# One layer of a state-space and pooling mixer on one core: the zero fill of the Toeplitz scratch placed behind the x loads, the pool groups from window 16 to window 2, and new places of issue

## The chip, the cores and the metric

The kernel runs on one core of a Trainium2 chip. Four engines compute: TensorE (PE, matmuls and transposes), VectorE (DVE), ScalarE (ACT) and GpSimd (POOL). SyncE (SP) issues every DMA of this kernel, in one queue. The metric is the device time of one execution in microseconds (us); less is better.

## What is computed

The reference is one layer with two mixers that read the same input. In short (2048 prompt rows and 8 sample rows of 1024 values, 512 columns to each mixer, 32 ssm groups of 16 channels with 64 complex states each):

```
proj = h @ w_in                                   # 1024 -> 2048
s_in, s_gate, p_in, p_gate = split(proj)          # 512 columns each
sy, hr, hi = s5_mixer(s_in, h0, ...)              # h_t = a*h_(t-1) + bbar*u_t ; y = Re(c*h) + d*u
sy = gelu(sy)
sy = sy * sigmoid(sy @ glu_w + glu_b)
py = pool_mixer(p_in, prefix)                     # per window w in (2, 4, 8, 16): mean of the last w rows
                                                  # minus the row; @ pool_w[group] ; * pool_scale
mixed = concat([sy * silu(s_gate), py * silu(p_gate)])
y = layer_norm(alpha * h + mixed @ w_out)
```

The outputs are y for the prompt and the sample rows, the new ssm states, and the last 15 rows of p_in.

## The kernel before

**Stages.** All large products are float32 products made of three passes of a high and a low part (hi by hi, hi by lo, lo by hi). x is loaded in 17 row tiles (`load_x`), transposed on PE and split into a high part `xh` (cast on ACT) and a low part `xl` (subtraction on DVE) by `put_x`. The in-projection `proj` (L200) makes 16 column tiles of 128: 0 to 3 are the ssm input (`u_tile`, L541), 4 to 7 its gates (`gate`), 8 to 11 the pool inputs (`pool_in`, L822) and 12 to 15 the pool gates (`pool_gate`). Each runs over chunks of 512 or 256 rows. `u_tile` copies its product on ACT to a tile `ue` and stores that to DRAM (`u_d`), from which the ssm stage reads it again by groups. There are two `ue` buffers, so the ACT copy waits until an earlier store has landed.

**The tables.** The state-space recurrence is done as block-Toeplitz products. The task `params` (L226) works the parameters up on DVE: exponentials, sines and cosines (tiles `tr`, `zs`), then powers (`prv`), and then eight blocks of two group pairs each (loop at L409). Each block has four products `sp` and two sums on DVE (L419 to L425), a PE part into `ps_ks` (L429 to L440, two small products and four transposes of `sp`), a split `sv` stored to `sw_d`, a sum `kf` split into `kv`, and a split `qh` stored to `qw_d`. After every second block eight DMAs write `kv` into `wt_d`, the Toeplitz scratch (L457 to L461). `wt_d` has to hold zeros in its other half, so `params` fills it before the blocks: a memset of the tile `wzero` on POOL and four DMAs of 1 MB (L375 to L380). The task `tables` (L464) makes the tables `tb` and `tx` for the ssm stage beside it. `ssm_task` (L678) waits until `params` and `tables` have ended, and then does 16 group pairs: it loads their tables and inputs, makes `uh`, and issues the products `s` and `y` on PE, with a scan on DVE (`B`, `hf`) and a copy on POOL (`bus`).

**The pooling.** For each of the four groups (tile numbers gi 0 to 3 have windows 2, 4, 8, 16) and each of five row chunks, `pool_in` puts the product into a tile `pc`, and the task `pool_diff` (L839) builds the sum over the window by doubling: log2(window) additions on POOL (tiles `ws`), then a difference `df` on DVE, and a split `dh` (cast on ACT, subtraction on DVE). `pool_gate` multiplies it on PE with the group's pool weights (`pm`) and stores the result to `mp_d`. The first three groups run beside the end of the ssm stage (loop at L925), the last one beside the GLU product `z` and the preparation of the output weights `wo` and of `mix`, the input of the output product `o`.

**What sets the order.** A hand-written order: each compute engine executes its instructions in the order in which the program records them. A class `Line` keeps a virtual clock; `proj` advances it after every three matmuls by the time they should take, and then lets every task run that is due. Tasks are generators, and `yield 3.0` says that the next piece is due 3.0 virtual us later. So the many numbers behind `yield`, and the start delays in `line.add`, decide only between which matmuls the next piece of work is recorded. The order of SP's DMAs is set by a scheduler from that program.

Of the kernel before, what the change touches and what calls it, by code (L numbers as in the profile page):

```python
# [17 lines left out]
P = 128  # L18
# [22 lines left out]
HT = HC // 2  # L41
CHUNKS_U = ((0, 256, 0), (256, 256, 0), (512, 512, 0), (1024, 512, 0), (1536, 256, 0), (1792, 256, NB))
# [60 lines left out]
def hybrid_step(  # L103
# [122 lines left out]
    def params(tmp, prod):  # L226
# [10 lines left out]
        yield 4.80  # L237
# [16 lines left out]
        yield 0.80  # L254
# [6 lines left out]
        def expo(out, z, shape, nm):  # L261
# [6 lines left out]
            yield 0.69  # L268
# [3 lines left out]
            yield 0.96  # L272
# [43 lines left out]
        yield 2.50  # L316
        V.tensor_scalar(out=acc, in0=r2, scalar1=-1.0 / math.factorial(14), scalar2=None, op0=ALU.mult)
        for i in (12, 10, 8, 6, 4, 2):
            if i == 6:
                yield 1.30  # L320
            V.scalar_tensor_tensor(out=acc, in0=acc, scalar=(-1.0) ** (i // 2) / math.factorial(i), in1=r2, op0=ALU.add, op1=ALU.mult)
        V.scalar_tensor_tensor(out=zs[:, 0], in0=acc, scalar=1.0, in1=sgn, op0=ALU.add, op1=ALU.mult)
        yield 2.50
# [23 lines left out]
        yield 0.84  # L347
# [19 lines left out]
        yield 1.00  # L367
# [7 lines left out]
        z = prod.tile([P, 512], F32R, tag="hl", name="wzero")  # L375
        G.memset(z.bitcast(F32), 0.0)
        for j in range(0, 8, 2):
            dma(out=wt_d[j:j + 2].rearrange("j a c g h o -> (j a c g h o)").rearrange("(p x o) -> p x o", x=4, o=512),
                in_=z.bitcast(F32).unsqueeze(1).to_broadcast([P, 4, 512]))
        yield 0.60  # L380
# [28 lines left out]
        for g0 in range(0, GP, N2):  # L409
# [17 lines left out]
            while not tabs:  # L427
                yield 0.50
# [28 lines left out]
            if (g0 + N2) % NG == 0:  # L457
                gs = slice(g0 + N2 - NG, g0 + N2)
# [4 lines left out]

    def tables():  # L464
        while "table" not in ready or "x" not in ready:
            yield 0.58
        zs = shared["zs"]
        for q in range(4):
# [3 lines left out]
            for lv in range(6):  # L472
# [6 lines left out]
                yield (1.20, 0.71, 0.79, 1.00, 0.74, 2.20)[lv]  # L479
            tx = tabs[0].tile([P, 2, 4, HT], F32, tag="tx", name=f"tx{q}")  # L480
            ms = tabs[0].tile([P, 2, 4, HT], F32, tag="mt", name="ms")
            for g in range(4):
# [4 lines left out]
                yield 0.60  # L487
# [87 lines left out]
    tab = line.add(tables(), 10.00)  # L575

    def x_task():
        for i in range(2, 17):
# [4 lines left out]
            yield 2.88 if i > 2 else 1.10  # L583
# [6 lines left out]
    xg = line.add(x_task(), 0.80)  # L590
# [18 lines left out]
    w3 = line.add(w_in_task(3, 2.48))  # L609
# [4 lines left out]
    line.add(w_in_task(4, 1.12))  # L614
# [63 lines left out]
    def ssm_task():  # L678
        while any(x[1] in (par, tab) for x in line.tasks):
            yield 0.09  # L680
# [13 lines left out]
        yield 0.51  # L694
# [4 lines left out]
        yield 2.40  # L699
# [69 lines left out]
        yield 5.86  # L769
# [52 lines left out]
    def pool_in(gi, c):  # L822
# [10 lines left out]
        ptasks.append(line.add(pool_diff(gi, c, pc), 0.14))  # L833
# [3 lines left out]
    def pool_diff(gi, c, pc):  # L837
# [9 lines left out]
        yield 0.98 + 1.22 * (len(bin(w)) - 3) * n / 512  # L847
# [24 lines left out]
    def pool_gate(gi, c):  # L872
        t0, n, s = c
        g = silu2(proj(12 + gi, c), n, s, f"p{gi}_{t0}")
        while (gi, t0) not in dfs:
            yield 0.24
# [6 lines left out]
        yield 1.00  # L883
# [15 lines left out]
    sg = line.add(ssm_task(), 0.50)  # L899
    gt = pw_sb = rcnt = sps = None  # L900
    for m in range(4):
# [6 lines left out]
        nxt = (6, 7, 8, 12)[m]  # L908
# [338 lines left out]
```

## Time and profile before

| | us |
|---|---|
| time, median of 3 runs | 711.62 (709.89 to 712.07) |
| the profiled execution's own time | 713.83 |
| its span in the trace | 711.9 |
| PE busy | 684.9 |
| DVE busy | 490.4 |
| ACT busy | 237.3 |
| POOL busy | 194.3 |
| mean granted clock of PE | 0.987 |

The busy time of an engine counts its instructions and not its waits, and it is a mean over stages with different limits. A table by stretches shows busy time, granted clock and DMA share for each stage; the waits of an engine say which instruction ended its idle time; a timeline shows single instructions, and in brackets how long the engine had stood idle before one and what released it.

### The profile page before, as it was taken

The numbers are of one execution on the slowest core, as the hardware profiler recorded it, in microseconds if no ns is written. First come the engines' busy times: TensorE is split into PE (matmuls) and PEld (weight loads), VectorE is DVE, ScalarE is ACT, GpSimd is POOL, SyncE is SP. The second block draws the span as 40 slices with busy tenths as digits, with TensorE's granted clock in tenths as the row PEclk, the third lists the DMA queues.
The fourth block names the chain that finished last, engine by engine and source line by source line (L and its number), as shares of the span: only waits on it lengthen the run. The fifth ranks groups of instructions, "written<-read, shape, count | busy, mean of one in ns | idle before, by whom it ended". The sixth has DMA issues, their size and how long they took to land.

```text
span 711.9 us, 10836 instructions
## 1 busy us (share of the span) xinstructions
PE 684.9 (96%) x3763; PEld 580.3 (82%) x3763; DVE 490.4 (69%) x1002; ACT 237.3 (33%) x490; POOL 194.3 (27%) x251
## 2 busy tenths in 40 slices
PE   7989889999999999999999999989999999999995
PEld 6978778878888888988987887776888868888884
DVE  3589989862665787687888973686655577666444
ACT  4244333331343343344334332363221323232100
POOL 0104554410000021022224213763314234153222
PEclk9999999999999999999999999999999999999998
DMA  8994477777654544344444325945354552752432
GB/s 252 289 333 111 112 190 206 170 211 216 189 159 137 162 132 125 111 146 142 127 145 129 107 90 133 358 138 106 103 120 121 112 143 74 177 160 72 111 88 59
DMA packets 138069, 107.95 MB, mean 152 GB/s; under 512 B 74467, under 2 KB 115591, under 8 KB 138007
## 3 DMA queue, kind: packets, MB, share of 16 engines
q1 hardware_dynamic: 137855, 107.01, 53.5%
q8 instruction: 29, 0.48, 0.3%
q10 hardware_dynamic: 160, 0.26, 0.1%
q14 instruction: 25, 0.20, 0.1%
HBM read 64.74 MB, written 42.73 MB: 151 GB/s over the span
## 4 chain that ended last, share of the span: by engine, by line
PE 71%; DVE 7%; ACT 3%; DMA 2%; SPq 2%; issue 1%; DVEq 0%; POOL 0%; ACTq 0%; POOLq 0%
PE pj L212 34%; PE o L1116 24%; PE z L1076 5%; PE y L669 2%; PE y L739 2%; PE s L654 2%; PE pm L880 1%; SPq L460 1%; PE os L1116 1%; DVE tx L486 1%; DMA wst<-in_w_in_dram 1%; DVE mix L150 1%; DVE wo L150 1%; DMA u_d<-ue 1%; DVE sp L150 1%
## 5 line engine op out<-in xcount | busy, mean ns | idle before, releaser
L212 PE MATMUL pj<-xh,w 128*128 128x512 f32 (+2 forms) x1312 | 335.4, 349 | 2.6 <-ACT w L156 2.6
L212 PEld LDWEIGHTS pj<-xh,w 128*128 128x128 f32 x1312 | 226.2, 191 | 32.6 <-ACT w L156 3.1
L212 PE MATMUL pj<-xl,w 128*128 128x512 f32 (+2 forms) x656 | 209.0, 350 | 0.0
L1116 PE MATMUL o<-wo,mix 128*128 128x512 f32 (+1 forms) x792 | 178.2, 386 | 1.5 <-ACT mix L156 1.5
L1116 PEld LDWEIGHTS o<-wo,mix 128*128 128x128 f32 x792 | 146.1, 189 | 32.7 <-ACT mix L156 2.5
L212 PEld LDWEIGHTS pj<-xl,w 128*128 128x128 f32 x656 | 121.7, 192 | 15.3
L150 POOL TENSOR_TENSOR xr<-xr,gb 128x1024 f32<-128x1024 f32 x15 | 37.0, 2470 | 48.5 <-DVE xr L150 35.5
L150 POOL TENSOR_TENSOR ws<-pc 128x527 f32<-128x527 f32 (+1 forms) x20 | 19.5, 977 | 106.5 <-ACT pc L831 57.9
L1076 PE MATMUL z<-yh,w_g 128*128 128x512 f32 (+2 forms) x240 | 45.1, 347 | 0.0
L1076 PEld LDWEIGHTS z<-yh,w_g 128*128 128x128 f32 x240 | 38.7, 189 | 5.9
L1105 ACT ACTIVATE xr<-xr,mv 128x1024 f32<-128x1024 f32 x15 | 18.7, 1244 | 74.2 <-DVE mv L1095 72.8
L713 POOL COPY bus<-SP 128x16 f32<-128x16 f32 x16 | 8.6, 535 | 119.9 <-ACT SP L707 119.8
L1084 DVE SCALAR_TENSOR_TENSOR xr<-xr,o 128x512 f32<-128x512 f32 (+1 forms) x33 | 22.0, 667 | 27.0 <-PE o L1116 27.0
L150 POOL TENSOR_TENSOR ws<-ws 128x525 f32<-128x525 f32 (+5 forms) x30 | 34.0, 1133 | 3.3 <-DVE dh L150 1.1
L150 DVE TENSOR_TENSOR xl<-pt,xh 128x1024 fp32r<-128x1024 f32 (+2 forms) x19 | 20.0, 1057 | 20.7 <-ACT xh L156 20.6
L150 DVE TENSOR_TENSOR yh<-y,yh 128x512 fp32r<-128x512 f32 (+2 forms) x20 | 13.9, 693 | 23.5 <-ACT yh L156 23.5
L150 POOL TENSOR_TENSOR mv<-mv,mhalf 128x1 f32<-128x1 f32 x16 | 9.9, 619 | 72.8 <-DVE mv L1090 69.5
L707 ACT COPY SP<-s 64x264 f32<-64x264 f32 x64 | 23.9, 373 | 17.3 <-PE s L654 16.8
L791 DVE SCALAR_TENSOR_TENSOR g<-g,pj 128x512 f32<-128x512 f32 (+1 forms) x20 | 11.6, 578 | 23.5 <-ACT g L790 23.5
L150 DVE TENSOR_TENSOR xr<-xr,gb 128x1024 f32<-128x1024 f32 x15 | 19.7, 1314 | 10.5 <-ACT xr L1105 10.5
L150 DVE TENSOR_TENSOR mix<-y,mix 128x512 fp32r<-128x512 f32 (+2 forms) x20 | 18.0, 901 | 12.7 <-ACT mix L156 12.7
L156 ACT CAST xh<-pt 128x1024 fp32r<-128x1024 f32 (+2 forms) x19 | 16.7, 884 | 26.4 <-PE pt L147 24.9
(222 smaller groups left out, 891.2 us busy)
## 6 DMA issues: line engine op xcount, KB each, us to landing
wst<-in_w_in_dram SPq DMA_DIRECT2D x15, 512.0 KB
xr<-in_x_prompt_dram SPq DMA_DIRECT2D x24, 256.0 KB
out_dram<-xr SPq DMA_DIRECT2D x22, 256.0 KB
xw<-in_x_prompt_dram SPq DMA_DIRECT2D x8, 512.0 KB
wt_d<-wzero SPq DMA_DIRECT2D x4, 1024.0 KB
sw_d<-sv SPq DMA_DIRECT2D x8, 512.0 KB
qw_d<-qh SPq DMA_DIRECT2D x16, 256.0 KB
ws<-sw_d SPq DMA_DIRECT2D x16, 256.0 KB
```

The lines of the kernel that those rows point to most:

```text
L150: (eng or V).tensor_tensor(out=out, in0=a, in1=b, op=op)
L156: S.copy(out=hi, in_=src)
L212: nc.tensor.matmul(out=ps[:, :n], lhsT=w[:, a, k], rhs=xcols(b, k, t0, n), start=(i == 0), stop=(i == 23))
L654: nc.tensor.matmul(out=ps[:, c, 0:264], lhsT=ws[:, c, a], rhs=uh[:, b, c, 8:272], start=(i == 0), stop=(i == 2))
L669: nc.tensor.matmul(out=py[:, c, 0:264], lhsT=wq[cs, r, a], rhs=hh[cs, b, r], start=False, stop=(i == 5))
L707: S.copy(out=SP[64 * c:64 * c + 64, a], in_=ps[64 * a:64 * a + 64, c, 0:264])
L739: nc.tensor.matmul(out=py[:, c, 0:264], lhsT=wt[:, c, a], rhs=uh[:, b, c, 0:264], start=(i == 0), stop=False)
L791: V.scalar_tensor_tensor(out=g[:, :n], in0=g[:, :n], scalar=1.0, in1=jm(ps[:, :n]), op0=ALU.add, op1=ALU.mult)
L1076: nc.tensor.matmul(out=ps[:, :n], lhsT=w[:, a, k, P * (m % 2):P * (m % 2) + P], rhs=yh[:, b, k, :n], start=(i == 0), stop=(i == 11))
L1084: V.scalar_tensor_tensor(out=xt[:n, c], in0=xt[:n, c], scalar=ALPHA, in1=ps, op0=ALU.mult, op1=ALU.add)
L1105: S.activation(out=xt[:n], in_=xt[:n], func=AF.Identity, scale=mv[:n, 2:3], bias=mv[:n, 0:1])
L1116: nc.tensor.matmul(out=ps, lhsT=lhs(a, k), rhs=wo_view(k)[:, b, 512 * h + c.start:512 * h + c.stop], start=(i == 0), stop=(i == len(hl) * ...
```

## The change

The change has three parts.

1. The zero fill is taken out of `params` and becomes a task of its own, `zeros`. It starts when all x tiles are put, takes its zero tile from a pool that is opened then, and issues the four fills 3.93 virtual us apart. The first `wt_d` write from `kv` waits (in the virtual order) for it, and `ssm_task` waits for its end.
2. The pool groups come in the order of `PG`: window 16, 8, 4, 2. The weights' loads follow that order, and the group beside the GLU product is now the one of window 2.
3. Some 45 numbers behind `yield` and of start delays are new.

```diff
+PG = (3, 2, 1, 0)
@@ params
-        z = prod.tile([P, 512], F32R, tag="hl", name="wzero")
-        G.memset(z.bitcast(F32), 0.0)
-        for j in range(0, 8, 2):
-            dma(out=wt_d[j:j + 2]..., in_=z...)
-        yield 0.60
+        yield 0.66
...
             while not tabs:
-                yield 0.50
+                yield 0.35
...
             if (g0 + N2) % NG == 0:
+                while "zeros" not in ready:
+                    yield 0.03
                 gs = slice(g0 + N2 - NG, g0 + N2)
...
+    def zeros():
+        while "x" not in ready:
+            yield 0.76
+        z = tabs[0].tile([P, 512], F32, name="wzero")
+        G.memset(z, 0.0)
+        for j in range(0, 8, 2):
+            dma(out=wt_d[j:j + 2]..., in_=z...)
+            yield 3.93
+        ready["zeros"] = True
...
-                yield (1.20, 0.71, 0.79, 1.00, 0.74, 2.20)[lv]
+                yield (1.11, 0.65, 0.70, 1.31, 0.74, 2.27)[lv]
...
-    PY = (5.08, 3.00, 2.20)
+    PY = (5.04, 3.00, 2.20)
...
+    zer = line.add(zeros(), 6.26)
-    tab = line.add(tables(), 10.00)
+    tab = line.add(tables(), 10.66)
...
-    w3 = line.add(w_in_task(3, 2.48))
+    w3 = line.add(w_in_task(3, 0.98))
...
-        while any(x[1] in (par, tab) for x in line.tasks):
+        while any(x[1] in (par, tab, zer) for x in line.tasks):
@@ pools
-        yield 0.98 + 1.22 * (len(bin(w)) - 3) * n / 512
+        yield 0.73 + 1.27 * (len(bin(w)) - 3) * n / 512
...
-        nxt = (6, 7, 8, 12)[m]
+        nxt = (6, 7, 8 + PG[0], 12 + PG[0])[m]
...
-    for gi in range(3):
+    for gi, ng in zip(PG, PG[1:]):
...
-    pool_seq(3, ((1, 0), (0, 0), (1, 1), ...), hook)
+    pool_seq(PG[3], ((1, 0), (0, 0), (1, 1), ...), hook)
@@ output stage
-        yield 5.43 if ck else 13.90
+        yield 13.07 if ck else 14.63
...
-            yield 2.70 if ck else 6.72
+            yield 0.14 if ck else 6.72
...
-        yield 7.00
+        yield 4.13
         yield from wo_split(1, (0, 1, 2, 3))
...
-            yield 0.83
+            yield 1.56
...
-    mb = line.add(mix_a(), 0.54)
+    mb = line.add(mix_a(), 1.31)
...
-    preps = {1: line.add(prep(1), 3.11)}
+    preps = {1: line.add(prep(1), 0.00)}
```

What it does to the order of the instructions shows at three places. The first is the queue of SP in the x stage and behind it (`xst` and `xw` are x tiles, `ue` the ssm input on its way to DRAM, `wst` an in-projection weight). Before, in the x stage:

```order
L521 DMA xst_277<-in_x_prompt_dram 128x1024
L378 DMA wt_d<-wzero 512x1x512
L521 DMA xst_318<-in_x_prompt_dram 128x1024
L548 DMA u_d<-ue_0_326 128x8x32
...
L548 DMA u_d<-ue_256_451 128x8x32
L378 DMA wt_d<-wzero 512x1x512
L521 DMA xst_475<-in_x_prompt_dram 128x1024
L521 DMA xst_497<-in_x_prompt_dram 128x1024
L378 DMA wt_d<-wzero 512x1x512
```

The same queue after the change, behind the x loads:

```order
L180 DMA wst_1075<-in_w_in_dram 128x8x128
L468 DMA wt_d<-wzero 512x1x512
L557 DMA u_d<-ue_1024_867 128x8x64
L557 DMA u_d<-ue_1536_910 128x8x32
L468 DMA wt_d<-wzero 512x1x512
L442 DMA sw_d<-sv 128x2x512
L557 DMA u_d<-ue_1536_967 128x8x32
L468 DMA wt_d<-wzero 512x1x512
```

The fills have moved from between x loads to between stores of `u_d` and of the first table block; the fourth comes six DMAs later. The second place is DVE at the last table block, before the change (`w` is the split of an in-projection weight, `g` a gate):

```order
L150 TENSOR_TENSOR kv_1785<-kf,kv_1785 32x2x128
L150 TENSOR_TENSOR qh<-qq,qh 128x4x128
L150 TENSOR_TENSOR w_1858<-wst_1811,w_1858 128x1024
L791 SCALAR_TENSOR_TENSOR g_512_1861<-g_512_1861,pj_512_1807 128x512
L150 TENSOR_TENSOR sp_1873<-bbar,prv_702 128x256
...
L150 TENSOR_TENSOR sp_1873<-sp_1873,sp_1874 128x256 x2
L791 SCALAR_TENSOR_TENSOR g_1024_1899<-g_1024_1899,pj_1024_1865 128x512
L150 TENSOR_TENSOR sv<-ps_ks,sv 128x4x128
```

And after it:

```order
L151 TENSOR_TENSOR kv_1779<-kf,kv_1779 32x2x128
L151 TENSOR_TENSOR qh<-qq,qh 128x4x128
L151 TENSOR_TENSOR sp_1859<-bbar,prv_688 128x256
...
L151 TENSOR_TENSOR sp_1859<-sp_1859,sp_1860 128x256 x2
L151 TENSOR_TENSOR w_1867<-wst_1811,w_1867 128x1024
L801 SCALAR_TENSOR_TENSOR g_512_1870<-g_512_1870,pj_512_1807 128x512
L151 TENSOR_TENSOR sv<-ps_ks,sv 128x4x128
L801 SCALAR_TENSOR_TENSOR g_1024_1914<-g_1024_1914,pj_1024_1874 128x512
```

The split of `w` and one `g` have moved from ahead of the block's `sp` to behind it. The third place is POOL at the first pool group, before the change (a name such as `ws_512_2` is the tile of the chunk from row 512, after the addition of distance 2):

```order
L827 MEMSET pc_0_2894 128x16
L150 TENSOR_TENSOR ws_0_1_2903<-pc_0_2894 128x527
L830 COPY pc_512_2945<-pc_0_2894 128x16
L150 TENSOR_TENSOR ws_512_1_2952<-pc_512_2945 128x527
L713 COPY bus<-SP_2967 128x16
```

And after it:

```order
L837 MEMSET pc_0_2897 128x16
L151 TENSOR_TENSOR ws_0_1_2904<-pc_0_2897 128x527
L151 TENSOR_TENSOR ws_0_2_2906<-ws_0_1_2904 128x525
L151 TENSOR_TENSOR ws_0_4_2908<-ws_0_2_2906 128x521
L151 TENSOR_TENSOR ws_0_8_2910<-ws_0_4_2908 128x513
L840 COPY pc_512_2957<-pc_0_2897 128x16
L151 TENSOR_TENSOR ws_512_1_2971<-pc_512_2957 128x527
L151 TENSOR_TENSOR ws_512_2_2973<-ws_512_1_2971 128x525
L151 TENSOR_TENSOR ws_512_4_2975<-ws_512_2_2973 128x521
L151 TENSOR_TENSOR ws_512_8_2977<-ws_512_4_2975 128x513
L723 COPY bus<-SP_2951 128x16
```

Each chunk of the first group now has four additions in a row on POOL ahead of the ssm stage's copy `bus`, where it had one.

## Rows read from the trace of the kernel before

**Rows 1.** The page: busy time by engine; the chain that ended last, by engine.

```profile
PE 684.9 (96%) x3763; PEld 580.3 (82%) x3763; DVE 490.4 (69%) x1002; ACT 237.3 (33%) x490; POOL 194.3 (27%) x251
PE 71%; DVE 7%; ACT 3%; DMA 2%; SPq 2%; issue 1%; DVEq 0%; POOL 0%; ACTq 0%; POOLq 0%
```

**Rows 2.** Waits of PE: line, waited for, us in total, times, longest.

```profile
PE ps_ks L147 <- DVE sp L150: 6.6, 5, 2.4
PE pm L880 <- ACT dh L156: 3.3, 3, 1.9
...
PE o L1116 <- ACT mix L156: 1.5, 2, 0.7
...
PE pm L880 <- DVE dh L150: 0.6, 3, 0.2
```

**Rows 3.** Stretches: PE, PEld, DVE, ACT, POOL busy, granted clock, DMA share, GB/s.

```profile
20.00:40.00 20.00, 19.95 (x145) 18.03 (x144) 13.50 (x45) 7.25 (x11) 0.87 (x11) 1.00 1.02 303
...
60.00:80.00 20.00, 17.64 (x116) 16.27 (x116) 19.05 (x45) 5.33 (x13) 14.57 (x24) 0.91 0.33 69
...
100.00:120.00 20.00, 18.86 (x105) 16.35 (x106) 18.25 (x58) 6.91 (x18) 8.54 (x14) 0.91 0.74 170
...
160.00:180.00 20.00, 19.73 (x100) 17.30 (x101) 5.42 (x13) 4.60 (x11) 0.59 (x2) 0.91 0.75 219
480.00:500.00 20.00, 18.51 (x70) 13.55 (x69) 13.28 (x17) 6.27 (x13) 6.30 (x5) 0.91 0.52 113
```

**Rows 4.** Timelines of the x stage: start, length, work [idle before, released by].

```profile
25.72 0.65 SPq L378 DMA_DIRECT2D wt_d<-wzero  x1
...
35.27 0.37 ACT L547 COPY ue<-pj 128x256 f32<-128x256 f32 x1 [5.16 <-DMA u_d<-ue]
...
36.59 2.36 DVE L150 TENSOR_TENSOR xl<-pt,xh 128x1024 fp32r<-128x1024 f32 x2 [1.94 <-ACT xh L156]
...
46.05 1.06 PE L147 MATMUL pt<-ident,xst 128*128 128x128 f32 x8 [2.08 <-DMA xst<-in_x_prompt_dram]
...
48.20 1.22 DVE L150 TENSOR_TENSOR xl<-pt,xh 128x1024 fp32r<-128x1024 f32 x1 [0.60 <-ACT xh L156]
```

**Rows 5.** Timeline of DVE: the four sp products of two table blocks.

```profile
69.68 3.46 DVE L150 TENSOR_TENSOR sp<-bbar,prv 128x256 f32<-128x256 f32 x4
...
109.27 1.43 DVE L150 TENSOR_TENSOR sp<-bbar,prv 128x256 f32<-128x256 f32 x4
```

**Rows 6.** Timelines of DVE and PE at the last table block.

```profile
156.59 1.23 DVE L150 TENSOR_TENSOR w<-wst,w 128x1024 fp32r<-128x1024 f32 x1 [2.47 <-ACT w L156]
157.73 0.68 DVE L791 SCALAR_TENSOR_TENSOR g<-g,pj 128x512 f32<-128x512 f32 x1
158.33 1.43 DVE L150 TENSOR_TENSOR sp<-bbar,prv 128x256 f32<-128x256 f32 x4
...
160.26 1.24 PE L147 MATMUL ps_ks<-ident,sp 128*128 128x128 f32 x4 [1.73 <-DVE sp L150]
...
179.38 0.72 DVE L150 TENSOR_TENSOR uh<-ut,uh 128x544 fp32r<-128x544 f32 x1 [5.18 <-ACT uh L156]
...
181.54 0.90 PE L654 MATMUL s<-uh,ws 128*128 128x264 f32 x6
```

**Rows 7.** Timelines of POOL and DVE in the last pool group.

```profile
451.41 4.81 POOL L150 TENSOR_TENSOR ws<-ws 128x525 f32<-128x525 f32 x3 [0.69 <-DVE dh L150]
...
476.44 4.60 DVE L150 TENSOR_TENSOR mix<-stage,mix 128x512 fp32r<-128x512 f32 x2
```

**Rows 8.** Stretches of the first three pool groups; POOL's additions there (busy, mean ns).

```profile
258.00:310.00 52.00, 52.00 (x325) 44.89 (x324) 40.02 (x84) 21.85 (x53) 5.92 (x12) 1.00 0.45 132
310.00:365.00 55.00, 55.00 (x334) 47.82 (x333) 45.30 (x90) 21.66 (x51) 12.84 (x18) 1.00 0.47 139
365.00:420.00 55.00, 54.74 (x336) 46.94 (x335) 48.28 (x87) 21.39 (x51) 18.92 (x24) 1.00 0.36 110
...
L150 POOL TENSOR_TENSOR ws<-ws 128x525 f32<-128x525 f32 (+3 forms) x15 | 15.3, 1018 | 1.2
```

More of the change, by code (lines that the diff above doesn't have):

```diff
@@ L253, in params @@
         transpose(ps[:, 64:72], ng, 8)
-        yield 0.80
+        yield 1.69
         lam = tmp.tile([P, 3, GP], F32, name="lam")
@@ L366, in params @@
         tt(q1, q1, den, ALU.mult)
-        yield 1.00
+        yield 0.77
         m1 = prod.tile([P, 2, GP, CH], F32, tag="p1", name="bm1")
@@ L462, in params @@
             yield PY[2]
+    def zeros():
[4 more added lines that the diff above has]
+        for j in range(0, 8, 2):
+            dma(out=wt_d[j:j + 2].rearrange("j a c g h o -> (j a c g h o)").rearrange("(p x o) -> p x o", x=4, o=512),
+                in_=z.unsqueeze(1).to_broadcast([P, 4, 512]))
+            yield 3.93
+        ready["zeros"] = True
     def tables():
         while "table" not in ready or "x" not in ready:
-            yield 0.58
+            yield 0.24
         zs = shared["zs"]
@@ L582, in x_task @@
             done.append(i)
-            yield 2.88 if i > 2 else 1.10
+            yield 2.88 if i > 2 else 1.65
         rx.close()
@@ L589, in hybrid_step @@
     done = [1]
-    xg = line.add(x_task(), 0.80)
+    xg = line.add(x_task(), 0.77)
     def need_x(i):
@@ L613, in hybrid_step @@
             line.finish(w3)
-    line.add(w_in_task(4, 1.12))
+    line.add(w_in_task(4, 1.10))
     for i, c in enumerate(CHUNKS):
@@ L693, in ssm_task @@
         ps = ssm_s(0)
-        yield 0.51
+        yield 0.43
         ph = bank("ps_h0")
@@ L698, in ssm_task @@
         S.copy(out=hs0.rearrange("p a b g -> p (a b g)"), in_=ph[:, 0:256])
-        yield 2.40
+        yield 2.50
         prev = None
@@ L768, in ssm_task @@
         tt(hsn, hsn, bus, ALU.add)
-        yield 5.86
+        yield 1.93
         ssm_out(*prev)
@@ L832, in pool_in @@
         pcs[gi] = (pc, n)
-        ptasks.append(line.add(pool_diff(gi, c, pc), 0.14))
+        ptasks.append(line.add(pool_diff(gi, c, pc), 0.00))
     dfs, gps = {}, {}
@@ L875, in pool_gate @@
         while (gi, t0) not in dfs:
-            yield 0.24
+            yield 0.84
         df = dfs.pop((gi, t0))
@@ L882, in pool_gate @@
         line.t += 0.64 * n / 512
-        yield 1.00
+        yield 1.04
         sl = gbT[:, 4 + gi:5 + gi]
@@ L897, in step_now @@
             pass
-    sg = line.add(ssm_task(), 0.50)
+    sg = line.add(ssm_task(), 0.00)
     gt = pw_sb = rcnt = sps = None
@@ L925, in hybrid_step @@
     PSEQ = ((0, 0), (0, 1), (1, 0), (0, 2), (1, 1), (0, 3), (1, 2), (0, 4), (1, 3), (1, 4))
-    for gi in range(3):
+    for gi, ng in zip(PG, PG[1:]):
         def hook(i, part):
             if (i, part) == (0, 0):
-                line.add(w_in_task(9 + gi))
+                line.add(w_in_task(8 + ng))
             if (i, part) == (4, 0):
-                line.add(w_in_task(13 + gi))
+                line.add(w_in_task(12 + ng))
         pool_seq(gi, PSEQ, hook)
@@ L937, in ssm_tail @@
         while any(x[1] is sg for x in line.tasks):
-            yield 0.37
+            yield 0.34
         right.close()
@@ L1010, in wo_split @@
                 wo_load(0, 2, 2, 0)
-            yield 4.12 if h else 1.12
+            yield 4.02 if h else 0.93
     def wo_a():
@@ L1102, in ln_tail @@
         mv = ln_scale(st, n, nm)
-        yield 2.50
+        yield 3.08
         ln_shift(mv, n)
         S.activation(out=xt[:n], in_=xt[:n], func=AF.Identity, scale=mv[:n, 2:3], bias=mv[:n, 0:1])
-        yield 0.99
+        yield 0.10
         tt(xt[:n], xt[:n], gb[:n, 0], ALU.mult)
-        yield 0.67
+        yield 0.58
         tt(xt[:n], xt[:n], gb[:n, 1], ALU.add, G)
@@ L1198, in hybrid_step @@
             new_mix(ck + 1)
-            pp = line.add(prep_pool(ck + 1), 1.24)
+            pp = line.add(prep_pool(ck + 1), 0.00)
         mix = mixes.pop(ck)
```

40 lines of the change are left out of this document (19 added, 21 removed).

## The prediction

> **What bounds the kernel now.** I read four views, in this order. The page's busy table and chain of waits come first [rows 1]: TensorE (PE) is busy 684.9 of 711.9 us, so 27.0 us are all that an edit of order alone can win, and part of that is start and tail. The waits of PE come next [rows 2]: beside the start and the tail they name four places, the transposes of the table blocks (ps_ks, 6.6 us in five waits for DVE), the pool product pm (3.3, for ACT's casts of the pool difference), the output product o (1.5, for the casts of mix) and one wait of 2.08 for an x tile, which stands in [rows 4]. The third view is the table by stretches [rows 3]. It adds a loss that no wait shows: a granted clock of 0.91 in 60 to 80, 100 to 120, 160 to 180 and 480 to 500 us, where PE had stood still or was sparsely fed before. Of the two levels, 2.4 and 1.2 GHz, the lower one then held for a part of the slice; 0.09 of 20 us is at most 1.8 us each. The same table says which engine sets the pace: DVE is busy 19.05 of 20 us in 60 to 80 and 18.25 in 100 to 120, so there DVE is the bound and PE waits for it. From 258 to 420 us PE is busy without a gap worth naming [rows 8], and an edit there can only lose. The fourth view, the timelines [rows 4 to 7], gives the price of single instructions.
>
> **The change part by part.** It adds and removes no arithmetic. So the sum is made of waits that go and waits that come. It is made against the profiled run (713.83 us, span 711.9), and carried over as a difference to the median of the runs, 711.62, which lies 2.21 below it.
>
> *1. The zero fill leaves the x loads.* Before, three of the four 1 MB fills were issued among the x loads (at 25.72 the first [rows 4]; by the order of SP the second and third stand directly around two x tiles), and the DMA engines are full there, share 1.02 in 20 to 40 us [rows 3]. With them went the 2.08 us that PE waited for an x tile at 46.05, ACT's 5.16 us in front of a copy to ue (at 35.27, for the landing of an earlier u_d store), and behind ACT four waits of DVE for xh: 1.94 at 36.59, 0.60 at 48.20 and two more like that one, some 3.6 in all [rows 4]. Without the fills the loads come earlier by up to 3 MB of a full queue, and these go. On PE the worth lies between 0 (the DVE chain refills the gap) and 2.08 + 3.6 = 5.7. I take 2.1, the wait that PE itself shows. The 3.6 of DVE shortens the chain that feeds ps_ks, but the new order also asks for some ps_ks transposes with less projection work ahead of them, and DVE has to be that much earlier to gain nothing.
>
> *2. The zero fill arrives later.* The four fills are now issued behind the x loads, 3.93 apart on the program's clock, among u_d stores and table stores. In 60 to 80 us the DMA share is 0.33 [rows 3], and 4 MB at the 303 GB/s of the full stretch are 13.8 us of all queues. What is queued behind a fill is the u_d store, and for its landing waits ACT's next ue copy, then ACT's casts, then DVE. The bounds are 0 (idle DMA takes it) and 5.16 for each of three fills, as in [rows 4], 15.5. I take 0.5, near the lower end, since the share of 0.33 is nearer to idle than 1.02 is. The write of kv that needs the zeros comes after the fourth block pair and finds them there; the new wait in the table task costs nothing while that holds. POOL's memset stands now before work that POOL reaches early anyway: 0.
>
> *3. The last table block.* In the order of DVE, the split of w and a g stand ahead of the last sp before, and behind it after. In the trace w starts at 156.59 after 2.47 of waiting for ACT, g follows at 157.73, sp at 158.33, and PE stands 1.73 in front of ps_ks at 160.26 [rows 6]. With sp first, DVE can begin it in that idle time, some 1.9 us (1.23 + 0.68) sooner, and PE's wait goes. With it goes the cause of the 0.91 in 160 to 180 [rows 3], at most 1.8. What comes late next is the first ssm product s at 181.54: its operand uh was written at 179.38 + 0.72 = 180.10, 1.4 us of slack [rows 6]. The chain to it (sv, kv, stores, loads back) now has the sw, gs and qw stores ahead of the kv stores on SP, and comes later against PE by about 1.9, hence 0.5 of new wait. The bounds are a loss of 0.5 and a gain of 1.7 + 1.8 = 3.5; I take 3.5 - 0.5 = 3.0.
>
> *4. The last pool group has window 2, not 16.* A pool difference for window 16 needs four POOL adds for each chunk, for window 2 one. Before, the last chunks' three adds behind the first took 4.81 us at 451.41, and with POOL reading the same memory DVE took 4.60 us for two splits of mix at 476.44 [rows 7]. PE paid 3.3 + 0.6 (a smaller group of pm waits, for DVE) in pm and 1.5 in o [rows 2], and a spell of 0.91 in 480 to 500 [rows 3]. With one add, all can go: 3.9 + 1.5 + 1.8 = 7.2; I leave 0.4 as a remnant. At the other end of the stage the window 16 comes first: fifteen adds more (three for each of five chunks) fall into the stretch that is about 258 to 310 us. At 1.02 us each [rows 8] that is 15.3 us of POOL, which has 46 us free there. What it costs PE is bounded by 0 and by 15.3 - 5.6 = 9.7 (rival B); I take 1.5, since DVE has 12.0 us idle in that stretch [rows 8] and PE's products there have slack. So 7.2 - 0.4 - 1.5 = 5.3.
>
> *5. The other numbers of issue.* They move prep, the wo splits and the LayerNorm steps by a few us. Those of the output stage move DVE and ACT work under PE's o products; the waits in [rows 2] show no loss there beyond the 1.5 already counted. I put it at 0, with 1 us either way. If that cover went, a wait of the size of o's two (0.75 each) [rows 2] for each of the five chunks would be 3.8.
>
> Sum: 2.1 - 0.5 + 3.0 + 5.3 + 0 = 9.9. The profiled run would be 713.83 - 9.9 = 703.9, the median 711.62 - 9.9 = 701.7. The ends of the terms for this case are 695.6 (parts 1 and 3 at their upper ends and no new waits: 5.7 + 3.5 + 6.8 = 16.0) and 706.5 (only half of the sum).
>
> **The rivals.**
>
> *A, slower: the fills hold up the u path.* The place is ACT's ue copy in 65 to 90 us. A 1 MB fill ahead of a u_d store delays its landing, ACT waits as at 35.27 (5.16), and the casts of the table blocks, kf and kv among them, queue behind on ACT; DVE, the bound there (19.05 of 20), follows one for one, and PE with it. Three fills at 5.16 are 15.5, and 701.7 + 15.5 = 717.2. It turns the result slower once the waits exceed 9.9, some 2.5 for each of four fills. For it speaks that DVE has nothing to spare there [rows 3], against it that the DMA share is 0.33. If ACT is kept for 2.5 or less a fill, it stays a small loss.
>
> *B: window 16 beside the ssm work slows DVE.* The row: four sp products took 3.46 us at 69.68 with POOL adds and memsets about, 1.43 at 109.27 with POOL idle [rows 5]. So POOL's adds can stop DVE. If each of the fifteen adds stops DVE for its whole 1.02 us, DVE has 15.3 us more in a stretch where it is busy 40.0 of 52; if all 12.0 idle can be used, 3.3 remain, with a clock spell 5.1, that is 3.6 more than I allowed: 705.3. If DVE can only be filled to the 88% that it has in 365 to 420 (48.28 of 55), its room is 5.6 and 9.7 remain, with the spell 11.5: 711.7. I take the middle, 708.5. Most of DVE's steps there read PSUM or one tile, which speaks against it. The Trainium skill, page "SBUF — State Buffer", section "Who interferes with whom", has this as a rule: a DVE instruction with two SBUF inputs and a GpSimd instruction that reads SBUF need the same pair of ports, and the second waits for the whole of the first. By that rule the time is this rival's; the rows of sp agree in direction, and the page would make the cost depend on how often the two meet.
>
> *C, no difference: the gaps come back.* PE is 96% busy. What is won at 46, 160 and 470 us can be lost again at the next wait for DVE, whose own work does not shrink: ps_ks waits at 74 and 100 us grow by the 2 us won, and the first ssm product by the 3. What is left of the last group's 5.3 then goes to the window-16 group. The time is 711.
>
> **How the numbers follow.** Main case (695.6 to 706.5) 0.62; B 0.14; C 0.09; A 0.15. A change of 0.3%, 2.1 us, is about what a measurement of this kernel can tell from none. Faster is the main case and most of B, 0.75; same is C and the upper end of B, 0.10; slower is A, 0.15. The range leaves out A beyond 713 and a small part below 695.
>
> **What would show it.** Right: no PE wait for an x tile, a ps_ks wait less at the eighth block and clock 1.00 in 160 to 180, pm and o waits of the last group gone with clock 1.00 in 480 to 500. Part 2 is wrong if ACT's waits for u_d between 60 and 100 us sum to over 5; part 4 if pm, y or s wait in the first pool group or DVE's steps there are longer; part 3 if the first s waits over 1 us. The whole is wrong if PE's idle time stays near 27, or if waits appear among the o products.

## The result and the profile after

| | before | after |
|---|---|---|
| median of the runs, us | 711.31 (709.89 to 712.07, 4 runs) | 704.14 (702.86 to 704.86, 4 runs) |
| profiled execution, us (span) | 713.83 (711.9) | 704.86 (703.1) |
| mean granted clock | 0.987 | 0.994 |

The ratio is 0.990, with a 95% interval from 0.9877 to 0.9922: 7.2 us faster, where 9.9 were forecast. The profiles of the two kernels lie 9.0 apart. The page of after, busy time by engine, as in [rows 1]:

```profile
PE 678.6 (97%) x3763; PEld 575.4 (82%) x3763; DVE 487.9 (69%) x1002; ACT 236.3 (34%) x490; POOL 192.9 (27%) x251
```

PE is 6.3 us less busy with the same 3763 matmuls, and its idle time is 24.5 us instead of 27.0. In the stretches below three slices fewer stand at 0.91, at most 1.8 us each, so that in this pair of profiles most of the gain looks like matmuls that ran at the higher clock, and not like idle time. (The last section shows how little the clock of one profile can bear.) The waits of PE after, as in [rows 2] (line, waited for, us in total, times, longest):

```profile
PE ps_ks L148 <- DVE sp L151: 6.8, 4, 3.1
...
PE pt L148 <- DVE xl L151: 1.2, 1, 1.2
PE pj L213 <- DVE gp L801: 0.9, 1, 0.9
PE o L1126 <- ACT mix L157: 0.7, 1, 0.7
```

The pm waits (3.3 and 0.6) have gone from the list and o has 0.7 instead of 1.5. But ps_ks waits as long as before. The stretches of after, in the columns of [rows 3]:

```profile
60.00:80.00 20.00, 20.00 (x139) 18.37 (x139) 19.19 (x51) 4.11 (x13) 15.13 (x25) 1.00 0.63 189
80.00:100.00 20.00, 13.73 (x68) 10.17 (x66) 17.34 (x47) 7.08 (x19) 11.75 (x18) 1.00 0.95 263
100.00:120.00 20.00, 20.00 (x110) 17.23 (x111) 16.00 (x57) 7.23 (x18) 6.28 (x10) 0.91 0.86 217
160.00:180.00 20.00, 20.00 (x111) 17.36 (x110) 5.96 (x12) 5.81 (x13) 0.59 (x2) 1.00 0.80 235
...
480.00:500.00 20.00, 19.12 (x80) 14.71 (x81) 11.12 (x22) 6.37 (x13) 2.69 (x6) 1.00 0.36 79
```

Of the four slices at 0.91 one is left, 100 to 120 us. The loss of PE in the tables' stretch is now gathered in 80 to 100 us (6.3 us). PE's timeline after, at the ps_ks products and at the first ssm product s:

```profile
84.54 0.92 PE L148 MATMUL ps_ks<-ident,sp 128*128 128x128 f32 x4 [2.29 <-DVE sp L151]
99.15 0.33 PE L148 MATMUL ps_ks<-ident,sp 128*128 128x128 f32 x1 [3.09 <-DVE sp L151]
...
177.43 0.89 PE L664 MATMUL s<-uh,ws 128*128 128x264 f32 x6
```

The first s starts 4.1 us earlier than in [rows 6] (181.54), and without a wait. A first reading would be that the forecast came true part by part (4.6 were forecast up to there). The experiments show that it did not: most of this gain belongs to another part of the change, the new numbers.

### The profile page after: what moved, and what is told of

Read it like the earlier page. It is cut to its first block, busy times and chain, and to the rows that moved or that the text cites. A ratio compares the mean times of both kernels' runs of the same rounds, so it can differ in the third digit from the quotient of the medians.

```text
span 703.1 us, 10834 instructions
## 1 busy us (share of the span) xinstructions
PE 678.6 (97%) x3763; PEld 575.4 (82%) x3763; DVE 487.9 (69%) x1002; ACT 236.3 (34%) x490; POOL 192.9 (27%) x251
## 4 chain that ended last, share of the span: by engine, by line
PE 74%; DVE 8%; ACT 2%; issue 1%; DMA 0%; DVEq 0%; SPq 0%; ACTq 0%
PE pj L213 37%; PE o L1126 24%; PE z L1086 5%; PE y L679 2%; PE s L664 1%; PE y L749 1%; DVE SP L151 1%; PE pm L890 1%; PE os L1126 1%; DVE mix L151 1%; DVE B L151 1%; DVE B L735 1%; DVE wo L151 1%; ACT SP L717 1%; PE ps_ks L428 1%
## 5 line engine op out<-in xcount | busy, mean ns | idle before, releaser
L213 PE MATMUL pj<-xl,w 128*128 128x512 f32 (+2 forms) x656 | 206.9, 347 | 0.0
L213 PEld LDWEIGHTS pj<-xl,w 128*128 128x128 f32 x656 | 120.0, 189 | 15.0
L717 ACT COPY SP<-s 64x264 f32<-64x264 f32 x64 | 23.9, 373 | 12.3 <-PE s L664 11.7
L157 ACT CAST xh<-pt 128x1024 fp32r<-128x1024 f32 (+2 forms) x19 | 16.8, 883 | 26.2 <-PE pt L148 24.7
L151 POOL TENSOR_TENSOR qp<-cc,pw 128x288 f32<-128x288 f32 x32 | 24.3, 789 | 0.6
L151 DVE TENSOR_TENSOR mix<-y,mix 128x512 fp32r<-128x512 f32 (+2 forms) x20 | 16.8, 838 | 10.4 <-ACT mix L157 10.4
```

The lines of the kernel that those rows point to most:

```text
L151: (eng or V).tensor_tensor(out=out, in0=a, in1=b, op=op)
L157: S.copy(out=hi, in_=src)
L213: nc.tensor.matmul(out=ps[:, :n], lhsT=w[:, a, k], rhs=xcols(b, k, t0, n), start=(i == 0), stop=(i == 23))
L717: S.copy(out=SP[64 * c:64 * c + 64, a], in_=ps[64 * a:64 * a + 64, c, 0:264])
```

## The experiments

Each kernel below ran in five rounds beside the kernel before, and the ratio is to that kernel, with its 95% interval. The kernel before came out at 709.9 to 711.4 beside the four groups of runs, so medians of different groups are comparable to about 1.5 us. All medians:

| run | what it is | median us | ratio (interval) |
|---|---|---|---|
| the change | late fill, groups reversed, new numbers | 704.14 | 0.9900 (0.9877 to 0.9922) |
| e1_fill_early | early fill, groups reversed, new numbers | 703.08 | 0.9879 (0.9852 to 0.9906) |
| e2_pg_up | late fill, old group order, new numbers | 707.64 | 0.9956 (0.9940 to 0.9971) |
| e11_numbers_alone | early fill, old group order, new numbers | 706.26 | 0.9932 (0.9915 to 0.9950) |
| e4_pg_alone | early fill, groups reversed, old numbers | 714.15 | 1.0053 (1.0032 to 1.0073) |
| e3_old_numbers | late fill, groups reversed, old numbers | 720.96 | 1.0138 (1.0113 to 1.0163) |
| e5_x_two_numbers | e3 and the x task's two numbers | 709.27 | 0.9981 (0.9958 to 1.0004) |
| e6_phase_one_number | e4 and one number of the ssm task | 708.86 | 0.9965 (0.9943 to 0.9987) |
| e7_tables_pause | the change, longer pause in the table task | 705.72 | 0.9924 (0.9897 to 0.9951) |
| e8_tables_spread | the change, table levels further apart | 705.58 | 0.9921 (0.9894 to 0.9948) |
| e9_early_fill_tables_pause | e1 and the longer pause | 703.45 | 0.9901 (0.9873 to 0.9928) |
| e10_early_fill_tables_later | e9 and a later start of the tables | 704.73 | 0.9928 (0.9902 to 0.9955) |
| e12_no_pool_products | the change without most POOL products of the tables | 699.03 | 0.9825 (0.9804 to 0.9846) |

### Which part brings the gain

**e1**, the fill put back, all else as changed (`wzero`, its memset and its four DMAs in `params`, no `zeros` task).

> The changed kernel with the zero fill put back among the x loads, all else as changed. By the prediction's terms (part 1 is worth 2.1 us, part 2 costs 0.5) it is 1.6 slower than the changed kernel, about 705.7, and the waits for an x tile (2.1) and of the ue copy for u_d (5) come back. Rival: the fill decides nothing, since DVE bounds the stretch from 60 to 140 us; then it is within 0.5 of 704.1. Second rival (the late fill costs more than the early one): 702 to 703.5.

703.08: not slower than the change. The two intervals overlap, so that by this pair alone the late fill is worth nothing, or costs up to some 2 us. Two pairs of runs further down differ by the same edit, e2 against e11 and e7 against e9. By their ratios the late fill costs 0.0024 and 0.0023, and here 0.0021, which is 1.5 to 1.7 us. In each of the three the intervals overlap; that they agree makes a small cost likely. Of the waits that were to come back with the early fill, the one for an x tile does not (0.74 in e1, 0.7 in the change). The one of the ue copy does in part (3.37 for 1.00), and PE does not feel it: the first product into ps_ks starts at 68.83 in e1 and at 69.17 in the change.

**e2**, only the group order put back:

```diff
-PG = (3, 2, 1, 0)
+PG = (0, 1, 2, 3)
```

> The changed kernel with the pool groups in the old order, window 2 to 16. By the prediction's term (5.3 us) about 709.4, with pm waits of 3 to 4 us between 430 and 475 us, two o waits and a lower granted clock near 490 us. Rival (what the last group loses the first wins back, as DVE is fuller there): within 1 of 704.1.

707.64, so that the reversed order is worth 3.5, not 5.3. The waits of PE in e2 show where (compare [rows 2]):

```profile
PE pm L890 <- ACT dh L157: 3.8, 3, 2.4
...
PE o L1126 <- ACT mix L157: 0.5, 1, 0.5
```

The pm waits come back as forecast, and so does a slice at 0.91 (columns of [rows 3], e2):

```profile
460.00:480.00 20.00, 16.56 (x82) 13.73 (x81) 16.62 (x22) 10.06 (x18) 12.62 (x10) 0.91 0.44 139
```

But o waits once and for 0.5, where the change itself keeps 0.9 (0.75 and 0.19 at its first o products), and the change pays 1.2 us of waits in its first group (0.30 and 0.87) that e2 doesn't have. 4.0 + 0.5 + 1.8 - 0.9 - 1.2 is 4.2 by the waits and the clock, with 1.8 as the most that the slice can cost; by the medians it is 3.5, and so it is between the two profiled executions (708.39 and 704.86).

**e11**, the kernel before with the new numbers alone.

> The kernel before with the new numbers of issue alone: fill among the x loads, groups from window 2 to 16. If the effects add up as in the runs so far (groups 3.5, fill -1.1, given the new numbers): 703.1 + 3.5 = 706.6, that is, the numbers alone bring 4 to 5 us of the 7.2. Rival (the numbers only serve the two structural edits): 710 to 712. The prediction put them at 0, apart from the last table block (3.0): 708.

706.26: the effects add up as the first theory of this run says. The numbers alone bring about 4.8 us (0.68%), and the prediction had put all of them but the last table block at 0. The first ssm product s shows where they bring it (timelines of PE, e11 and then e1; 181.54 in [rows 6]):

```profile
176.20 0.90 PE L655 MATMUL s<-uh,ws 128*128 128x264 f32 x6
```

```profile
176.25 0.90 PE L655 MATMUL s<-uh,ws 128*128 128x264 f32 x6
```

That is 5.3 us earlier than before, with the fill still among the x loads, and 1.2 earlier than in the change. PE has no wait for an x tile in e11, and ACT's wait for an u_d store, 5.16 in [rows 4], is 1.99 (timeline of ACT, e11):

```profile
32.82 0.37 ACT L548 COPY ue<-pj 128x256 f32<-128x256 f32 x1 [1.99 <-DMA u_d<-ue]
```

So with the new numbers the fill among the x loads costs PE nothing that the traces show, and the waits of [rows 4] shrink without the fill being moved.

### With the old numbers both edits cost time

**e4**, the kernel before with `PG` and nothing else.

> The kernel before with the pool groups reversed and nothing else. By the prediction's term 711.3 - 5.3 = 706.0, the pm and o waits of the last group gone. Rival: without the new numbers the window-16 group holds PE up beside the ssm work (pm, y or s waits of 2 us or more between 250 and 310 us): 708 to 711.

714.15, slower than before: the rival B of the prediction, in the place that it named. PE waits 1.08 for uh and 2.00 for hh (the split of hf, an input of y). The timelines of PE, DVE and POOL in e4 beside each other:

```profile
272.69 0.88 PE L655 MATMUL s<-uh,ws 128*128 128x264 f32 x5 [1.08 <-DVE uh L151]
278.98 0.51 PE L670 MATMUL y<-hh,wq 64*128 64x264 f32 x4 [2.00 <-ACT hh L157]
...
272.55 1.55 DVE L151 TENSOR_TENSOR SP<-B,tbl 128x512 f32<-128x512 f32 x1
274.14 1.44 DVE L151 TENSOR_TENSOR B<-B,tbl 128x512 f32<-128x512 f32 x1
275.61 2.60 DVE L151 TENSOR_TENSOR hf<-SP,B 128x256 f32<-128x256 f32 x2
...
280.49 0.69 DVE L151 TENSOR_TENSOR B<-SP,tbl 128x512 f32<-128x512 f32 x1 [0.82 <-ACT SP L708]
281.28 0.69 DVE L151 TENSOR_TENSOR SP<-SP,tbl 128x512 f32<-128x512 f32 x1
282.01 0.76 DVE L151 TENSOR_TENSOR SP<-SP,B 128x256 f32<-128x256 f32 x2
...
273.64 4.29 POOL L151 TENSOR_TENSOR ws<-ws 128x525 f32<-128x525 f32 x3
```

While POOL adds for the window of 16, from 271.9 on, DVE's steps SP, B and hf take 1.55, 1.44 and 2.60 (SP is here a tile, and not the engine). They are the last steps ahead of hh, for which the product y waits. At the other end, what the reversed order was to save mostly stays: the pm waits are 2.7 for 3.9, those of o 1.5 as before (waits of PE, e4), and the slice of 480 to 500 us is at 0.91 again:

```profile
PE pm L881 <- ACT dh L157: 1.6, 2, 1.2
PE o L1117 <- ACT mix L157: 1.5, 2, 0.8
...
PE pm L881 <- DVE dh L151: 1.1, 2, 0.9
```

**e6**, e4 with one number changed. In the order of POOL and DVE it moves the ssm chain ahead, to where the change has it:

```diff
-        yield 2.40
+        yield 0.90
         prev = None
```

> The old kernel with reversed pool groups (714.15), with one number changed: the wait of the ssm task before its first group pair, 2.40 to 0.90. In the order of POOL and DVE this moves the ssm chain 1.5 us ahead against the pool groups, to where the changed kernel has it. Theory (POOL's four additions double the DVE steps that they meet; before, these were the last steps ahead of the product y, in the changed kernel earlier ones with slack): PE's waits of 1.1 for uh and 2.2 for hh at 272 and 279 us go, with the lower clock (0.97) in 260 to 310: 714.15 - 3.3 - 1.5 = about 709.4, while DVE's busy time in the stretch stays the same. Rival (it is the amount of DVE work, 46 of 55 us, that fills the stretch): the waits move to other products, 713 or more.

708.86, 5.3 less than e4, where the theory had 4.8. The same steps in e6:

```profile
270.50 0.68 DVE L151 TENSOR_TENSOR SP<-B,tbl 128x512 f32<-128x512 f32 x1
271.21 0.69 DVE L151 TENSOR_TENSOR B<-B,tbl 128x512 f32<-128x512 f32 x1
271.94 0.76 DVE L151 TENSOR_TENSOR hf<-SP,B 128x256 f32<-128x256 f32 x2
...
275.46 1.43 DVE L151 TENSOR_TENSOR B<-SP,tbl 128x512 f32<-128x512 f32 x1 [1.29 <-ACT SP L708]
276.99 1.36 DVE L151 TENSOR_TENSOR SP<-SP,tbl 128x512 f32<-128x512 f32 x1
278.38 1.75 DVE L151 TENSOR_TENSOR SP<-SP,B 128x256 f32<-128x256 f32 x2
...
275.27 4.24 POOL L151 TENSOR_TENSOR ws<-ws 128x525 f32<-128x525 f32 x3
```

The three steps take 0.68, 0.69 and 0.76, and it is the first steps of the next group pair that meet POOL (1.43 and 1.36 for what takes 0.69 alone). All eight instructions shown take 7.7 us in e4 and 6.7 in e6: most of the slowed work did not go, it moved to where PE doesn't wait for it. Of the gain, 3.2 us have arisen by the end of the first pool group (the transpose pq starts at 298.49 for 301.67), with PE's waits of 1.08 and 2.00 gone and a clock of 1.00 for 0.97 in 260 to 310 us. The rest comes behind 420 us, where e4 has a pm wait of 1.15 and the slice at 0.91 and e6 has neither; the theory did not name those.

**e3**, both structural edits with the old numbers.

> The late fill and the reversed pool groups, with all numbers of issue as before the change. By the prediction's term for the last table block (3.0 us) about 707.1, with the ps_ks wait of 1.7 and the lower clock in 160 to 180 us back. Rival: the numbers were worth more than that block, through the ssm and output stages: 709 or more, with waits after 250 us that the changed kernel doesn't have. Rival: they are worth nothing, 704.

720.96, far slower than before. The waits after 250 us that the second theory names are there, but e4 has them too. By the medians e3 lies 6.8 above e4. Its profiled execution lies 4.6 above that of e4, and in it the first s starts 5.9 later, at 184.58 for 178.70, so that the loss arises ahead of the ssm stage. The timelines of SP, ACT and PE in e3:

```profile
84.44 0.84 SPq L468 DMA_DIRECT2D wt_d<-wzero  x1
85.38 0.65 SPq L557 DMA_DIRECT2D u_d<-ue  x1
86.08 1.63 SPq L180 DMA_DIRECT2D wst<-in_w_in_dram  x1
...
72.51 0.37 ACT L556 COPY ue<-pj 128x256 f32<-128x256 f32 x1 [5.69 <-DMA u_d<-ue]
93.04 1.05 ACT L157 CAST w<-wst 128x1024 fp32r<-128x1024 f32 x1 [11.18 <-DMA wst<-in_w_in_dram]
...
101.86 1.49 PE L428 MATMUL ps_ks<-qq,bd 128*32 128x128 f32 x6 [5.91 <-ACT qq L408]
```

This is the prediction's rival A, with one difference. The u_d wait that it named is there (5.69 at 72.51), but the costlier one is the load of an in-projection weight (`wst`) that is queued behind the last fill, where e4 issues it at 63.52: ACT stands 11.18 us in front of its cast, and everything behind that on ACT, the scaling of qq among it, makes PE wait 5.91. In the x stage itself e3 does gain what the prediction's part 1 says: it has no wait for an x tile where e4 has 1.11, an u_d wait of 2.56 for 5.26, the first product into ps_ks starts at 68.25 for 69.11, and the transposes of that block at 70.24 for 72.52.

**e5**, e3 with two numbers of the x task:

```diff
-            yield 2.88 if i > 2 else 1.10
+            yield 2.88 if i > 2 else 1.65
-    xg = line.add(x_task(), 0.80)
+    xg = line.add(x_task(), 0.77)
```

> The late fill and the reversed groups with the old numbers (720.96), but with the two numbers of the x task as changed (start 0.77, first step 1.65). In the order of SP this alone puts the load of the in-projection weight of tile 3 ahead of the four fills; with the old two it is behind them, issued at 86.08 in the trace. Theory (the late fill costs what is queued behind it, here that weight): ACT's wait of 11.2 us for the weight and PE's wait of 5.9 at 101.9 go, with the part of the low clock in 100 to 120 us that follows; 720.96 - 5.9 - 2 = about 713. Rival (the fills' traffic itself holds the stretch up): 719 or more, with the 5.9 spread over other waits.

709.27, 11.7 less than e3 where 8 were expected. In the queue of SP the weight is now ahead of all fills, as in the change (timeline of SP, e5):

```profile
61.92 0.37 SPq L180 DMA_DIRECT2D wst<-in_w_in_dram  x1
67.41 0.65 SPq L468 DMA_DIRECT2D wt_d<-wzero  x1
```

The wait of 5.91 is gone, though PE now waits longer for sp in the same place (timeline of PE, e5; 2.05 in e3):

```profile
100.40 1.24 PE L148 MATMUL ps_ks<-ident,sp 128*128 128x128 f32 x4 [4.63 <-DVE sp L151]
```

The first s starts at 177.86, no later than in e4 with its early fill. The fills' traffic is the same as in e3, so that the price was not the traffic; the weight that is queued behind it is the cause that fits, with ACT's 11.18 in front of it. These two numbers change more than the one load, since e5 is also 4.9 below e4. What the rest is was not taken apart; in the traces the waits for uh and hh in the first pool group, 1.08 and 1.98 in e3, are 0.29 and 0.24 in e5, as they are in e6.

### What the tables' stretch hangs on

The remaining ps_ks waits (6.8 us) are the largest wait of PE in the change. The first theory was that table levels stand ahead of sp on DVE. **e7** lengthens the pause between two quarters of the tables, **e8** the distance of the levels:

```diff
-            yield 6.31
+            yield 11.30
```

> The changed kernel with the pause of the table task between two quarters 11.30 instead of 6.31, so that a quarter goes with two table blocks. Theory (in 80 to 140 us DVE is late because table levels stand ahead of sp): of the 6.8 us of ps_ks waits 3 or more go and the low clock in 100 to 120 as well (1.8): 699 to 701, with a later end of the tables hidden, as DVE has room from 140 us on. Rival (DVE's sum decides, the waits move to the next block): within 1 of 704.1.

> The changed kernel with the table levels themselves 1.6 times as far apart (and 0.80 for 0.55), the pause unchanged, so that the same quarter takes some 20 us. Theory as for the longer pause: 699 to 701. If the place of the levels ahead of sp decides and not their rate, this one and the longer pause differ by over 1 us. Rival: within 1 of 704.1.

Both are no faster than the change, 705.72 and 705.58. In e8, too, a wait for sp remains, 3.49 at 122.90. In e7 the wait at 99.15 has gone, but another of 2.86 and 0.49 appears at 123 us, and two slices are at a lower clock (0.83 in 80 to 100, 0.91 in 120 to 140 us). ACT has a long wait ahead of it (timeline of ACT, e7):

```profile
111.74 0.37 ACT L556 COPY ue<-pj 128x256 f32<-128x256 f32 x1 [6.79 <-DMA u_d<-ue]
```

**e9** is the same pause with the early fill, and **e10** starts the tables 1.5 us later on top of it, which puts the sp of the first and of the third block ahead of their quarter's first levels in the order of DVE.

> The changed kernel with the fill back among the x loads (703.08) and, on top, the longer pause of the table task, 11.30, that brought nothing beside the late fill (705.7). Theory (there the pause failed because the late fills, kv and qw stores kept the DMA queue full: ACT waited 6.8 us for an u_d store at 111.7, and sp came late behind it): without the late fill that wait is under 3 us, the ps_ks waits at 97 and 122 us (1.3 and 2.4) and the low clock in 120 to 140 us (1.8) go: 698 to 700. Rival (DVE's own sum over 60 to 140 us decides): 702 to 705.

> The same as the kernel with early fill and longer pause, and the table task starts 1.5 us later, which puts the sp of the first three table blocks ahead of any table level in the order of DVE. Theory (a level ahead of sp costs PE what it lasts): 0.5 to 1.5 us less than the kernel with the pause alone. Rival (the order inside the block is hidden by the 5 us between sp and ps_ks): the same within 0.5.

703.45 and 704.73: neither beats e1 (703.08). ACT's wait for the u_d store is still there in e9, 6.77 at 111.06 without any late fill, so that the fill is not its cause. e10 could not show much: the two blocks that it changes have no ps_ks wait in e9, and its waits are those of the second and the sixth block, which e9 has too (3.30 at 85.06 and 2.42 at 135.32, for 2.28 and 2.29). What stays is the rival, that DVE's sum decides, not its order. **e12** takes a part of that sum away without touching the order: for seven of the eight table blocks POOL's products and sums are left out, and their result is filled with zeros, so that e12 does not compute the whole layer.

```diff
+            if g0 > 0:
+                G.memset(Q, 0.0)
+                qs[g0] = Q, bd
+                return
```

> The changed kernel with POOL's products and sums for the table blocks 2 to 8 (tiles qp and qq, 35 us of POOL in 66 to 146 us) left out and their result filled with zeros; the output part that hangs on them is wrong. DVE's order is the same, instruction by instruction. Theory (the ps_ks waits come from DVE's two-input steps being slowed by POOL, as the sp products at 3.46 against 1.43): in 66 to 140 us sp, tb, mt and tx fall to the lengths that they have with POOL idle, some 16 us less in sum, the ps_ks waits fall from 6.8 to under 1.5 and the low clock in 100 to 120 us goes: 704.1 - 5.3 - 1.8 = about 697. Rival (the order of the steps or the DMA stores make sp late): ps_ks waits of 5 or more and 702 to 704.

699.03, 5.1 us below the change (7.1 were expected). The stretch 66 to 140 us of the change and then of e12 (the line of both that holds the stretch's sums):

```profile
66.00:140.00 74.00, 66.78 (x393) 56.37 (x392) 64.76 (x192) 24.56 (x63) 38.88 (x64) 0.98 0.82 219
```

```profile
66.00:140.00 74.00, 70.91 (x413) 60.18 (x412) 52.61 (x201) 27.11 (x70) 10.68 (x30) 0.98 0.90 242
```

DVE gets through nine more instructions in 12.2 us less. Its groups there (busy, mean ns), of the change and then of e12:

```profile
L151 DVE TENSOR_TENSOR tb<-mt 128x8 f32<-128x8 f32 (+5 forms) x46 | 13.0, 324 | 0.8
L151 DVE TENSOR_TENSOR mt<-tb,zs 128x32 f32<-128x32 f32 (+5 forms) x44 | 12.7, 330 | 0.6
L151 DVE TENSOR_TENSOR sp<-bbar,prv 128x256 f32<-128x256 f32 x24 | 12.2, 566 | 0.0
```

```profile
L151 DVE TENSOR_TENSOR sp<-bbar,prv 128x256 f32<-128x256 f32 x28 | 10.7, 445 | 0.0
L151 DVE TENSOR_TENSOR mt<-tb,zs 128x32 f32<-128x32 f32 (+5 forms) x44 | 9.2, 250 | 0.6
L151 DVE TENSOR_TENSOR tb<-mt 128x16 f32<-128x16 f32 (+5 forms) x44 | 7.1, 204 | 0.8
```

The ps_ks waits fall from 6.8 to 3.0. Of these, 2.31 at 94.78 has another cause: there DVE itself had waited 2.03 us for a store of a table (timeline of DVE, e12),

```profile
85.23 0.06 DVE L483 MEMSET tb<- 128x4 f32 x1 [2.03 <-DMA tb_d<-tb]
```

and it is followed by a slice at 0.91 (80 to 100 us). That would account for the 2 us by which the expectation missed; it was not tried apart. So about 5 us of the change's time is the price of POOL's products in this stretch; that they act through DVE is what the shorter steps say, since PE's own wait for qq, which comes of POOL's products, is only 0.35 in the change.

## Why the prediction was right, and which steps of it were not

The direction held, the time lies in the range (704.14 for 701.7), and 7.2 us came of 9.9. The steps fared unequally: what the prediction left out made up for much of what it had too large, and that is luck.

**Part 1, the fill leaves the x loads, 2.1: wrong for this change.** The mechanism exists: with the old numbers the first table block comes 0.9 to 2.3 us earlier without the fill (e3 beside e4). The step that failed is to count it beside the new numbers. With these PE loses nothing to the fill in its old place (e11, e1), whose waits are smaller or hidden there. The 2.08 was also a large sample: in e4, whose instructions are those of the kernel before up to there, the x tiles' waits were 1.1 and 0.5. The lower bound of 0 was right.

**Part 2, the late fill costs 0.5: small as forecast in the change, right in mechanism as rival A.** With the new numbers the late fill costs about 1.5 (three pairs of runs, in each of which the intervals overlap). With the old ones it costs 6.8 (e3 over e4). What keeps it cheap is, as far as e5 shows, that the weight's load stands ahead of the fills, which two numbers of the x task bring about. The prediction looked at u_d stores and not at the weight loads in the same queue, though the row with `wst` ahead of the first fill stood in its own order of SP.

**Part 3, the last table block, 3.0: right in place.** At the last block's ps_ks PE has no wait, 160 to 180 us is at 1.00, and s doesn't wait. The clock term is not shown: in e4 the last block's wait is 1.98 and the slice behind it is at 1.00 all the same. And what was won at the last and at the first block (1.73 at 160.26 and 2.35 at 74.12 before) was lost again at the second and third (2.29 at 84.54 and 3.58 at 99.15, for none and 2.19 before): rival C, inside this stretch. That s nevertheless starts 4.1 earlier is the numbers' doing (e11).

**Part 4, window 2 last, 5.3: right in mechanism beside the new numbers, too large.** 3.5 (e2). The pm and clock terms were right there (4.0 and a slice at 0.91 come back in e2), o's was not: e2 has 0.5 of it and the change 0.9, where 1.5 and 0.4 were in the sum. Its ground was misread: the 4.60 for two splits of mix in [rows 7] ran beside splits that POOL itself did then, and not beside the window's additions, the last of which ended at 470.74 (timeline of POOL, before):

```profile
467.02 3.72 POOL L150 TENSOR_TENSOR ws<-ws 128x269 f32<-128x269 f32 x3 [0.42 <-DVE dh L150]
476.33 2.45 POOL L150 TENSOR_TENSOR wo<-stage,wo 128x1024 fp32r<-128x1024 f32 x1 [5.59 <-ACT wo L156]
478.75 3.44 POOL L150 TENSOR_TENSOR mix<-stage,mix 128x512 fp32r<-128x512 f32 x2
```

With the old numbers the o waits stay under the reversed order (e4). The 1.5 allowed for the first group came out as 1.2 in the profile. That it is not 5 or more there is again the numbers' doing: with the old ones the reversed order is a loss of 3.3 (e4), and one number turns it (e6). The remark under rival B that most of DVE's steps there read PSUM or one tile was wrong; the steps on SP, B and hf, which were slowed, each read two tiles in SBUF.

**Part 5, the other numbers, 0: wrong, and the main error.** They are worth about 4.8 alone (e11), of which the prediction had 3.0 in part 3. With both structural edits in place, they are worth 16.8 (720.96 to 704.14). The prediction saw in them a few moves in the output stage; alone their worth lies ahead of the ssm stage (first s at 176.20 for 181.54), and beside the structural edits in two queues as well, SP at 60 to 90 us and POOL against DVE at 260 to 300 us.

By parts, then: the numbers 4.8 for 3.0, the group order 3.5 for 5.3, the fill -1.1 for +1.6, in sum 7.2 for 9.9. One more step was loose: the difference was formed on a profiled execution that lay 2.5 us above the median of before, where that of after lies 0.7 above its own. On the two profiles the change is 9.0.

No tried version beats the change clearly. e1, the change with the fill put back, is 1.1 us faster by medians, and the intervals overlap. e12 shows where more is to be had: POOL's table products, moved to where DVE isn't the bound.

## What to carry to other kernels

Where an edit comes with new places of issue, look in each in-order queue for what the moved work now stands ahead of: here the same 4 MB of fill cost some 1.5 us or 7, depending on what was queued behind it, and one place of issue that decided which DVE steps the same POOL additions met was worth 5 us, some 3 of them in that stretch. A wait that ends on a moved transfer is not the transfer's price; only the kernel with that one part undone tells, and with all other parts as they will be. And where the engine that is the bound is slowed by another one's work, take away that work before reordering the first one's: four edits of order brought nothing here.

## What the runs showed of the hardware

A DVE step with two inputs in SBUF takes about twice its time, and sometimes more, while POOL runs additions or products that read SBUF: 1.44 against 0.69 for B, 2.60 against 0.76 for two hf (e4, e6), and a mean of 324 ns against 204 for the tb steps, six shapes in nearly the same mix, with and without POOL's products (the change, e12). The Trainium skill, page "SBUF — State Buffer", section "Who interferes with whom", says that such a pair contends, since the second input comes through the read interface that DVE shares with GpSimd, and calls the shared ports an exclusive lock. The rows agree that DVE is slowed; how the two take turns they don't show.

The lower clock did not follow the length of the wait alone. The same wait of 2.28 or 2.29 us for sp near 84 us was followed by a slice at full clock in the change, e1 and e2 (1.00 in 80 to 100 us), and by one at 0.91 in e9 and e11 and 0.83 in e7. The order of the instructions cannot be what made the difference: e1 and e11 differ only in the order of the pool groups, which begin later, and are among the two kinds. Nor did the lower clock cost anything there: e1 at full clock came earlier to the third block and waited 1.27 for its sp, e11 had no wait, and the first s starts at 176.25 and 176.20. So a slice at 0.91 in one profile is not yet a loss where DVE is the bound.
